# FFN up projection as seven products of halves, activations through DRAM, in a hybrid decoder layer on one NeuronCore

## The chip, the cores and the metric

The kernel runs on one core of a Trainium2 chip. The metric is device time in microseconds of one execution, the median of several runs. TensorE (PE) multiplies, VectorE (DVE) and ScalarE (ACT) do element-wise work, GpSimd (POOL) small scalars and some DMA issues, SyncE (SP) most DMA issues.

## The reference, cut

One decoder layer on 1024 tokens and 1024 channels in float32. Two sub-layers (a token mixer and a cross-attention into 256 memory tokens) come first and are not changed. The third is a gated MLP with a causal convolution of width 3 over the tokens:

```python
def conv_ffn(h, w_up, conv_w, conv_b, w_down):
    z = h @ w_up                                   # (1024 x 1024) @ (1024 x 5632)
    zc = conv_w[2] * z + conv_w[1] * shift_right(z, 1) + conv_w[0] * shift_right(z, 2) + conv_b
    g, u = zc[..., :D_FF], zc[..., D_FF:]          # D_FF = 2816
    return (jax.nn.gelu(g, approximate=True) * u) @ w_down

h = rms_norm(x, ffn_pre_g[l])
x = x + rms_norm(conv_ffn(h, w_up[l], conv_w[l], conv_b[l], w_down[l]), ffn_post_g[l])
```

## The kernel before

Every float32 product is made of three float32r matmuls: an operand is split into a rounded high part (`split`, L100, on ScalarE) and the rest (L101, on VectorE), and high x high, high x low and low x high are summed in PSUM.

The normalised activations are transposed to channels x tokens (`xtrans`, L894, through `transpose_pair`) into four tiles `h3` of the pool `hp`, a high and a low one for each half of the tokens. The pool has four buffers, and the cross-attention's output weights `woh`, `wol` hold two of them until its last product. The transposes of the last quarter of the tokens, `xtrans(3)`, come between the first up products (L975).

The up projection (L963 to L985) runs over j = 0 to 21, 128 gate columns and the 128 matching up columns of `w_up` each. `wload` fetches and splits a 128 x 1024 weight tile in the order of the list `stream`; `feature_major` (L226) multiplies it with both halves of the tokens over eight k tiles. The gate goes to one of two wide PSUM tiles, the up part to two of four banks. `conv_wide` and `conv` read PSUM: ScalarE makes the first tap and the bias, VectorE adds the other two. A gelu on ScalarE and a product on VectorE (L984, L985) give `act[j]`, and all 22 stay in SBUF in slots of the pool `ap` (28 slots of 4 KB per partition, shared by everything).

The down projection (L995 to L1176) already runs as seven products of halves (Strassen's scheme in Winograd's form): the tokens' halves, the halves of the 2816 and of the 1024 output columns. A step is one product and one of its eleven k tiles, 4 x 3 matmuls of 512 columns. `load` (L1032) fetches `w_down` four steps ahead, `prepare` (L1049) makes the sums and the split operands two steps ahead, `products` (L1082) issues the matmuls, `evacuate` empties the accumulators. The first two steps (HEAD = 2, L999) use tiles of the front pools; then these pools are closed (L1011) and the pool `dp` takes their place, so its tiles wait until their users are done.

The program text gives priorities; a planner in the framework orders each engine's queue by these and by when it expects inputs, so neighbouring instructions can change places. DMAs on one issuing queue start in order.

Of the kernel before, what the change touches and what calls it, by code (L numbers as in the profile page):

```python
# [16 lines left out]
P = 128  # L17
# [21 lines left out]
def hybrid_kernel(ctx, tc, out, x, xT, g_col, mem, gains, b_forget, w_fm, w_v0, w_v1, pool_w, pool_scale,  # L39
# [10 lines left out]
    ps = ctx.enter_context(tc.tile_pool(name="ps", bufs=4, space=bass.MemoryType.PSUM))  # L50
# [45 lines left out]
    def f32(a):  # L96
        return a.bitcast(F32)
# [20 lines left out]
    for j in range(NJ):  # L118
        stream += [w_up[j], w_up[NJ + j]]
# [772 lines left out]
    h3 = []  # L892

    def xtrans(q4, k2s=range(4)):  # L894
        if len(h3) <= q4 // 2:
            h3.append((hslot(), hslot()))
        c0 = (q4 % 2) * 256
        transpose_pair(yrs[q4], lambda k2: tuple(h3[q4 // 2][j][:, 2 * k2:2 * k2 + 2, c0:c0 + 256]
                                                 for j in range(2)), k2s, g_cols[:, 2])
# [21 lines left out]

    filler = xqueries(1)
    ox = xattend(0, lambda i: step(filler, 5))
    step(filler, 99)
    for q4 in range(4):
        units = xout(q4, ox)
        if q4 < 3:
            ox = xattend(q4 + 1, lambda i: step(units, 1))
        else:
            step(units, 6)  # L930
        if 0 < q4:
            xtrans(q4 - 1, (0, 1))
        step(units, 1)
        if 0 < q4:
            xtrans(q4 - 1, (2, 3))
        step(units, 9)


    act = [slot(s="act") for _ in range(NJ)]
    cg = [slot(s="cg") for _ in range(2)]  # L940

    ring(q=(0, 1), u=(2, 3, 0, 1))

    def conv(dst, o, m, hf, zt):

        w0, w1, w2 = (cwt[:, i, m:m + 1] for i in range(3))
        b, d = o[hf], dst[:, hf * 512:(hf + 1) * 512]
        nc.scalar.activation(d, b, AF.Identity, bias=cbt[:, m:m + 1], scale=w2)
        nc.vector.scalar_tensor_tensor(d[:, 1:], b[:, :511], w1, d[:, 1:], ALU.mult, ALU.add)
        nc.vector.scalar_tensor_tensor(d[:, 2:], b[:, :510], w0, d[:, 2:], ALU.mult, ALU.add)  # L950
        if hf == 0:
            nc.vector.tensor_copy(zt, b[:, 510:512])
        else:
            nc.vector.scalar_tensor_tensor(d[:, 0:1], zt[:, 1:2], w1, d[:, 0:1], ALU.mult, ALU.add)
            nc.vector.scalar_tensor_tensor(d[:, 0:2], zt, w0, d[:, 0:2], ALU.mult, ALU.add)

    def conv_wide(dst, b, m):
        w0, w1, w2 = (cwt[:, i, m:m + 1] for i in range(3))
        nc.scalar.activation(dst, b, AF.Identity, bias=cbt[:, m:m + 1], scale=w2)
        nc.vector.scalar_tensor_tensor(dst[:, 1:], b[:, :S - 1], w1, dst[:, 1:], ALU.mult, ALU.add)  # L960
        nc.vector.scalar_tensor_tensor(dst[:, 2:], b[:, :S - 2], w0, dst[:, 2:], ALU.mult, ALU.add)

    for j in range(NJ):  # L963
        gt, ut = cg[j % 2], act[j]
        wg = wload()
        wu = wload()
        og = wbank()
        ou = [bank("u"), bank("u")]
        zt = small(2, s="zt")
        if j == 0:  # L970
            for hf in range(2):
                feature_major(wg, h3, halves(og), (hf,))
                feature_major(wu, h3, ou, (hf,))
                if hf == 0:
                    xtrans(3)  # L975
                conv(ut, ou, NJ + j, hf, zt)
            conv_wide(gt, og, j)
        else:
            feature_major(wg, h3, halves(og))
            conv_wide(gt, og, j)  # L980
            feature_major(wu, h3, ou)
            for hf in range(2):
                conv(ut, ou, NJ + j, hf, zt)
        nc.scalar.activation(gt, gt, AF.Gelu_apprx_tanh)  # L984
        nc.vector.tensor_mul(ut, ut, gt)  # L985
# [5 lines left out]

    HEAD = 2  # L995
    operands = {}
    raw = new_raw().rearrange("p (k n) -> p k n", k=2)
    nc.sync.dma_start(out=raw, in_=w_down[0:2 * P, 0:512].rearrange("(k p) n -> p k n", p=P))
    for i in range(HEAD):  # L999
        o = []  # L1000
        for src in (act[i][:, :512], raw[:, i]):
            hi, lo = (wp.tile([P, 512], F32R, tag=t, name=nm(t), bufs=4) for t in ("wh", "wl"))
            split(hi, lo, src)
            o.append((hi, lo))
        operands[i] = o
        for t in range(4):
            tt = slice(t * P, (t + 1) * P)
            for n, (l, r) in enumerate(((0, 0), (0, 1), (1, 0))):
                nc.tensor.matmul(halves(wide[t // 2])[t % 2], o[0][l][:, tt], o[1][r], start=n == i == 0,
                                 stop=False, skip_group_check=True)  # L1010
# [6 lines left out]
    def residual(tg):  # L1017
# [8 lines left out]
    raws = {}  # L1026
    sums_a, sums_b = [], []

    NEEDS = {"p1": ((0, 0), (0, 1)), "p5": ((1, 1),), "p6": (), "p3": ((1, 1),),
             "p7": ((1, 1), (0, 1)), "p2": ((1, 0),), "p4": ()}  # L1030

    def load(i):  # L1032

        p, k = steps[i]
        if k % 2:
            return
        n = min(2, NK - k)
        for q in NEEDS[p]:
            r = dslot("wd", bufs=4)
            r0 = (q[0] * NK + k) * P  # L1040
            nc.sync.dma_start(out=r[:, :n], in_=w_down[r0:r0 + n * P, q[1] * 512:(q[1] + 1) * 512]
                              .rearrange("(k p) n -> p k n", p=P))
            for kk in range(n):
                raws[p, k + kk, q] = r[:, kk]

    def quarter(a, b, k):
        return act[b * NK + k][:, a * 512:(a + 1) * 512]

    def prepare(i):  # L1049

        p, k = steps[i]
        w = [raws.pop((p, k, q)) for q in NEEDS[p]] or [None]
        a11, a12, a21, a22 = (quarter(i, j, k) for i in range(2) for j in range(2))
        if p == "p1" and k % 2 == 0:
            sums_a.append(dslot("sa"))
            sums_b.append(dslot("sb"))
        s_, t_ = sums_a[k // 2][:, k % 2], sums_b[k // 2][:, k % 2]
        if p == "p7":
            nc.vector.tensor_tensor(w[0], w[0], w[1], ALU.subtract)
        a, b = {"p1": (a11, w[0]), "p5": (s_, t_), "p6": (s_, t_), "p3": (s_, w[0]),  # L1060
                "p7": (s_, w[0]), "p2": (a12, w[0]), "p4": (a22, t_)}[p]
        if i >= HEAD:
            o = [dslot("o", F32R) if i < tail else slot((P, 2, 512), F32R, s="ot") for _ in range(2)]
            split(o[0][:, 0], o[0][:, 1], a)
            split(o[1][:, 0], o[1][:, 1], b)
            operands[i] = o
        if p == "p1":
            nc.vector.tensor_tensor(s_, a21, a22, ALU.add)
            nc.vector.tensor_tensor(t_, w[1], w[0], ALU.subtract)
        elif p == "p5":  # L1070
            nc.vector.tensor_tensor(s_, s_, a11, ALU.subtract)
# [5 lines left out]
        elif p == "p2":  # L1077
            nc.vector.tensor_tensor(t_, w[0], t_, ALU.subtract)
# [165 lines left out]
```

## Time and profile before

| | |
|---|---|
| runs | 1552.12, 1557.56, 1558.25 us, median 1557.56 |
| profiled execution | 1554.77 us, span 1553.0 us |
| TensorE busy | 1514.1 us (97%) |
| VectorE busy | 893.8 us (58%) |
| ScalarE busy | 630.5 us (41%) |
| DMA | 131.17 MB, mean 84 GB/s |

The busy time of overlapping, pipelined matmuls says that TensorE has work, not that it runs at its peak; the spacing of matmul starts tells their pace. The up projection lies from about 840 to 1322 us of the span, the down projection behind it.

### The profile page before, as it was taken

How to read it: one execution, taken by the hardware profiler on the slowest of the kernel's cores; microseconds unless marked ns; L12 is line 12 of the kernel's file. 1: busy time of each engine (PE TensorE's matmuls, PEld its weight loads, DVE VectorE, ACT ScalarE, POOL GpSimd, SP SyncE). 2: the span in 40 equal slices, each digit the busy share in tenths (PEclk: the TensorE clock that was granted, in tenths of full speed). 3: DMA queues.
4: the chain of work that ended last, by engine and by line, in shares of the span. 5: the costliest groups of instructions: out<-in, count | busy, mean ns of one | idle time of the engine just before them, and what ended most of it. 6: DMA issues, size and time to landing. Idle time of an engine off the chain costs nothing. (4 is left out here: it accounts for less than half of the span.)

```text
span 1553.0 us, 19127 instructions
## 1 busy us (share of the span) xinstructions
PE 1514.1 (97%) x7316; PEld 1256.4 (81%) x7316; DVE 893.8 (58%) x1414; ACT 630.5 (41%) x1176; POOL 118.4 (8%) x270
## 2 busy tenths in 40 slices
PE   7999999999999999999999999999999999899997
PEld 7888888878888888877888888888888888688885
DVE  7578777663233444676565534444344444886786
ACT  6356555232122233554677322222232222354453
POOL 4000000000000000033022000000000000000003
PEclk9999999999999999999999999999999999899999
DMA  5244332111122125354222111111111111522622
GB/s 166 80 109 104 90 89 69 58 37 49 45 65 74 48 88 183 101 181 153 82 101 91 54 41 55 45 51 54 41 55 41 55 43 39 186 79 85 193 89 108
DMA packets 50315, 131.17 MB, mean 84 GB/s; under 512 B 6192, under 2 KB 6640, under 8 KB 50224
## 3 DMA queue, kind: packets, MB, share of 16 engines
q1 hardware_dynamic: 41824, 100.30, 21.7%
q0 software_dynamic: 8256, 29.40, 5.5%
q8 instruction: 57, 0.93, 0.3%
q14 instruction: 34, 0.28, 0.1%
q10 hardware_dynamic: 144, 0.26, 0.0%
HBM read 104.61 MB, written 12.75 MB: 76 GB/s over the span
## 5 line engine op out<-in xcount | busy, mean ns | idle before, releaser
L100 ACT ACTIVATE wh<-wr 128x512 fp32r<-128x512 f32 x214 | 134.0, 630 | 496.6 <-PE wide L235 292.4
L101 DVE TENSOR_TENSOR wl<-wr,wh 128x512 fp32r<-128x512 f32 x214 | 146.4, 689 | 306.2 <-ACT wh L100 306.0
L233 PE MATMUL wide<-h,wh 128*128 128x512 f32 x608 | 189.3, 390 | 0.9 <-ACT h L223 0.4
L237 PE MATMUL wide<-h,wl 128*128 128x512 f32 x608 | 189.2, 389 | 0.5 <-DVE wl L101 0.5
L235 PE MATMUL wide<-h,wh 128*128 128x512 f32 x608 | 189.0, 390 | 0.1
L233 PEld LDWEIGHTS wide<-h,wh 128*128 128x128 f32 x608 | 113.8, 188 | 25.6 <-ACT wh L100 0.7
L237 PEld LDWEIGHTS wide<-h,wl 128*128 128x128 f32 x608 | 114.1, 188 | 24.6 <-DVE wl L101 0.9
L235 PEld LDWEIGHTS wide<-h,wh 128*128 128x128 f32 x608 | 114.1, 188 | 24.4 <-DVE h L224 0.5
L1089 PE MATMUL wide<-o,o 128*128 128x512 f32 x456 | 106.9, 396 | 7.0 <-ACT o L100 6.9
L233 PE MATMUL bank<-h,wh 128*128 128x512 f32 x352 | 109.8, 389 | 0.0
L237 PE MATMUL bank<-h,wl 128*128 128x512 f32 x352 | 109.7, 389 | 0.0
L235 PE MATMUL bank<-h,wh 128*128 128x512 f32 x352 | 109.6, 389 | 0.0
L1089 PEld LDWEIGHTS wide<-o,o 128*128 128x128 f32 x456 | 87.2, 191 | 26.2 <-ACT o L100 7.3
L1089 PE MATMUL bank<-o,o 128*128 128x512 f32 x396 | 90.8, 390 | 0.0
L1089 PEld LDWEIGHTS bank<-o,o 128*128 128x128 f32 x396 | 74.1, 188 | 16.3 <-DVE o L101 0.9
L164 PE MATMUL bank<-h,wh 128*128 128x512 f32 x192 | 77.0, 401 | 1.3 <-DVE qk L442 1.3
L235 PEld LDWEIGHTS bank<-h,wh 128*128 128x128 f32 x352 | 66.1, 188 | 13.7
L237 PEld LDWEIGHTS bank<-h,wl 128*128 128x128 f32 x352 | 66.1, 188 | 13.7
L233 PEld LDWEIGHTS bank<-h,wh 128*128 128x128 f32 x352 | 66.1, 188 | 13.7
L165 PE MATMUL bank<-h,wh 128*128 128x512 f32 x192 | 76.0, 396 | 0.0
L166 PE MATMUL bank<-h,wl 128*128 128x512 f32 x192 | 75.8, 395 | 0.0
L101 DVE TENSOR_TENSOR pt<-bank,pt 128x512 fp32r<-128x512 f32 (+2 forms) x96 | 50.8, 550 | 11.0 <-ACT pt L100 10.7
(316 smaller groups left out, 2946.2 us busy)
## 6 DMA issues: line engine op xcount, KB each, us to landing
wr<-in_w_up SPq DMA_DIRECT2D x44, 512.0 KB
wd<-in_w_down SPq DMA_DIRECT2D x35, 512.0 KB
wr<-in_w_fm SPq DMA_DIRECT2D x28, 512.0 KB
wr<-in_w_mix_out SPq DMA_DIRECT2D x16, 512.0 KB
qs<-qk SPq DMA_DIRECT2D x32, 128.0 KB
kd<-qk SPq DMA_DIRECT2D x32, 128.0 KB
xr<-in_x POOLq DMA_DIRECT2D x8, 512.0 KB, 6.3
x1d<-xr POOLq DMA_DIRECT2D x8, 512.0 KB, 3.4
```

Of the source, the lines that this page charges most:

```text
L100: nc.scalar.activation(hi, src, AF.Copy)
L101: nc.vector.tensor_tensor(lo, src, f32(hi), ALU.subtract)
L164: nc.tensor.matmul(o, lh, rh, start=start, stop=False)
L165: nc.tensor.matmul(o, lh, rl, start=False, stop=False)
L166: nc.tensor.matmul(o, ll, rh, start=False, stop=stop)
L233: nc.tensor.matmul(o[h], wh[:, ks], hT[h][0][:, k], start=st, stop=False)
L235: nc.tensor.matmul(o[h], wh[:, ks], hT[h][1][:, k], start=False, stop=False)
L237: nc.tensor.matmul(o[h], wl[:, ks], hT[h][0][:, k], start=False, stop=sp)
L1089: nc.tensor.matmul(o, oa[:, l, tt], ob[:, r], start=n == k == 0 and p in ("p1", "p5", "p2"), stop=n == 2 and k == NK - 1, skip_group_check ...
```

## The change

The up projection gets the scheme that the down projection has. For each j, the 2 x 2 blocks are: gate or up columns, halves of the 1024 input channels, halves of the tokens. Seven products of a 128 x 512 weight block with a 512 x 512 activation block take the place of eight. The weight sums s1 to s4 are made by VectorE for each j (`prepare_up`, four products ahead); the activation sums t1 to t4 are made once (`b_sums`), in two quarters, from the right half's raw transposes `raws_b`, while p1 and p2 of the first three j, which need the left half only, run first. PSUM is laid out anew as eight banks, three for X (p1, p6, p7, p4 of one j accumulate there), three for p2, two for p5 and p3. Products are emptied by ScalarE (p1, p5, p6, p4) or added by VectorE (p3, p7, p2) into SBUF tiles, and the convolution reads those. `act[j]` and, for each pair, the sum of its right halves are written to DRAM on the POOL queue; the down projection loads the quarter it needs, pairs of neighbouring j being its two halves.

```diff
-    for j in range(NJ):
-        stream += [w_up[j], w_up[NJ + j]]
...
+    FILL = 3
+    up_steps = [(j, p) for j in range(FILL) for p in ("p1", "p2")]
+    for j in range(NJ):
+        up_steps += [(j, p) for p in ("p5", "p6", "p3", "p7")]
+
+        if j > 0:
+            at = up_steps.index((j, "p5")) + (1 if j < FILL else 0)
+            up_steps.insert(at, (j - 1, "p4"))
+        if j >= FILL:
+            up_steps.append((j, "p2"))
+        if FILL <= j + 1 < NJ:
+            up_steps.append((j + 1, "p1"))
+    up_steps.append((NJ - 1, "p4"))
+    LEAD_UP = 4
...
+    def prepare_up():
...
+        if name == "s1":
+            nc.vector.tensor_tensor(s_, a["a21"], a["a22"], ALU.add)
+        elif name == "s2":
+            nc.vector.tensor_tensor(s_, s_, a["a11"], ALU.subtract)
+        elif name == "s4":
+            nc.vector.tensor_tensor(s_, a["a12"], s_, ALU.subtract)
+        elif name == "s3":
+            nc.vector.tensor_tensor(s_, a["a11"], a["a21"], ALU.subtract)
+        hi, lo = up_ops[n % 6]
+        split(hi, lo, a.get(name, s_))
...
+    def b_sums(q4):
+
+        c = slice((q4 % 2) * 256, (q4 % 2) * 256 + 256)
+        r12, r22 = raws_b[q4]
+        t_ = slot((P, 4, 256), s="tr")
+        b11, b21 = quarters["b11"], quarters["b21"]
+        nc.vector.tensor_tensor(t_, r12, f32(b11[:, :4, c]), ALU.subtract)
+        nc.vector.tensor_tensor(t_, t_, f32(b11[:, 4:, c]), ALU.subtract)
+        b_split(q4, "t1", t_)
+        yield
+        nc.vector.tensor_tensor(t_, r22, t_, ALU.subtract)
+        b_split(q4, "t2", t_)
+        yield
+        b_split(q4, "b22", r22)
+        yield
+        nc.vector.tensor_tensor(r12, r22, r12, ALU.subtract)
+        b_split(q4, "t3", r12)
+        yield
+        nc.vector.tensor_tensor(t_, f32(b21[:, :4, c]), t_, ALU.subtract)
+        nc.vector.tensor_tensor(t_, t_, f32(b21[:, 4:, c]), ALU.add)
+        b_split(q4, "t4", t_)
+        yield
...
+    def product_up(n):
+        j, p = up_steps[n]
+        o = {"p5": UY[j % 2], "p3": UY[j % 2], "p2": UZ[j % 3]}.get(p, UX[j % 3])
...
+        for k in range(4):
+            ks = slice(k * P, (k + 1) * P)
+            for i, (l, r) in enumerate(((ah, bh), (ah, bl), (al, bh))):
+                nc.tensor.matmul(o, l[:, ks], r[k // 2][:, k % 2], start=i == k == 0 and p in ("p1", "p5", "p2"),
+                                 stop=i == 2 and k == 3, skip_group_check=True)
...
+    def pair_done(j):
+
+        d = conv_wide(z[j][1], NJ + j)
+        nc.vector.tensor_mul(d, d, gates.pop(j))
+        nc.gpsimd.dma_start(out=act_d[j], in_=d)
...
+        if j % 2:
+            s_ = slot((P, 512), s="sd")
+            nc.vector.tensor_tensor(s_, act_ring.pop(j - 1)[:, right], act_ring.pop(j)[:, right], ALU.add)
+            nc.gpsimd.dma_start(out=sum_d[j // 2], in_=s_)
...
+    plan = {0: ((2, 1),), 1: ((2, 2),), 2: ((3, 1),), 3: ((3, 1),), 4: ((3, 1),), 5: ((2, 1), (3, 1)), 6: ((2, 1), (3, 1))}
...
+    for n in range(len(up_steps)):
+        j, p = up_steps[n]
+        if n == 2:
+            xtrans(3)
+        product_up(n)
+        for q4, m in plan.get(n, ()):
+            step(sums[q4], m)
+        prepare_up()
...
-    HEAD = 2
+    HEAD = 4
...
+    LOADS = {"p1": ("a11", "b11"), "p5": ("s", "b12"), "p6": ("b22", "a12"), "p3": ("b22", "a21"),
+             "p7": ("b22", "b12"), "p2": ("b21",), "p4": ("a22",)}
...
+            if q == "s":
+                r = dslot("sa")
+                for kk in range(n):
+                    nc.sync.dma_start(out=r[:, kk], in_=sum_d[k + kk])
+            elif q[0] == "a":
+                r = slot((P, 2, 512), s=q)
+                c = slice((int(q[1]) - 1) * 512, int(q[1]) * 512)
+                for kk in range(n):
+                    nc.sync.dma_start(out=r[:, kk], in_=act_d[2 * (k + kk) + int(q[2]) - 1][:, c])
```

## Rows read from the trace of the kernel before

**Rows 1.** The page: busy time, share and instructions by engine; granted clock by slice.

```profile
PE 1514.1 (97%) x7316; PEld 1256.4 (81%) x7316; DVE 893.8 (58%) x1414; ACT 630.5 (41%) x1176; POOL 118.4 (8%) x270
...
PEclk9999999999999999999999999999999999899999
```

**Rows 2.** Windows, up then down: length, busy by engine (count), clock, DMA share, GB/s.

```profile
1000.00:1100.00 100.00, 100.00 (x443) 82.79 (x442) 44.42 (x62) 27.76 (x37) 0.00 (x0) 1.00 0.16 48
...
1360.00:1400.00 40.00, 40.00 (x178) 33.13 (x177) 34.27 (x55) 20.86 (x38) 0.00 (x0) 1.00 0.23 73
1400.00:1500.00 100.00, 100.00 (x441) 82.08 (x440) 77.77 (x127) 50.00 (x94) 4.31 (x8) 1.00 0.43 137
```

**Rows 3.** Timeline, up projection: start, duration, engine, line; one j apart.

```profile
1082.75 0.62 PE L233 MATMUL wide<-h,wh 128*128 128x512 f32 x2
...
1104.51 0.62 PE L233 MATMUL wide<-h,wh 128*128 128x512 f32 x2
```

**Rows 4.** Timeline of TensorE: hand-over, then whole products of the down projection.

```profile
1322.11 0.39 PE L1009 MATMUL wide<-wh,wh 128*128 128x512 f32 x1
...
1334.59 27.63 PE L1089 MATMUL wide<-o,o 128*128 128x512 f32 x108 [6.88 <-ACT o L100]
...
1362.05 30.08 PE L1089 MATMUL bank<-o,o 128*128 128x512 f32 x132
1391.97 30.08 PE L1089 MATMUL wide<-o,o 128*128 128x512 f32 x132
```

**Rows 5.** Instructions by line and form, down projection: busy us, mean ns, idle before.

```profile
L101 DVE TENSOR_TENSOR o<-sa,o 128x512 fp32r<-128x512 f32 x43 | 29.7, 690 | 18.1 <-ACT o L100 18.1
...
L1076 DVE TENSOR_TENSOR sa<-act 128x512 f32<-128x512 f32 x11 | 7.5, 684 | 0.0
...
L1113 DVE TENSOR_TENSOR y<-y,bank 128x512 f32<-128x512 f32 x4 | 2.5, 678 | 0.0
...
L100 ACT ACTIVATE o<-sa 128x512 fp32r<-128x512 f32 x43 | 27.2, 632 | 60.9 <-PE bank L1089 30.9 <-PE wide L1089 29.8
...
L1105 ACT ACTIVATE y<-wide 128x512 f32<-128x512 f32 x4 | 2.2, 589 | 0.2 <-PE wide L1089 0.2
```

**Rows 6.** Instructions by line and form, up projection, 880 to 1320.

```profile
L961 DVE SCALAR_TENSOR_TENSOR cg<-wide,cwt,cg 128x1022 f32<-128x1022 f32 x21 | 26.9, 1281 | 0.8
...
L985 DVE TENSOR_TENSOR act<-act,cg 128x1024 f32<-128x1024 f32 x20 | 24.5, 1226 | 0.7
L959 ACT ACTIVATE cg<-wide,cbt,cwt 128x1024 f32<-128x1024 f32 x20 | 23.8, 1191 | 0.0
L984 ACT ACTIVATE cg<-cg 128x1024 f32<-128x1024 f32 x21 | 22.3, 1061 | 57.5 <-DVE cg L961 57.5
```

**Rows 7.** Timeline of VectorE in the down projection: consecutive instructions.

```profile
1369.57 0.68 DVE L1071 TENSOR_TENSOR sa<-sa,act 128x512 f32<-128x512 f32 x1
...
1370.17 0.68 DVE L1072 TENSOR_TENSOR sb<-wd,sb 128x512 f32<-128x512 f32 x1
```

**Rows 8.** Timeline of TensorE: first up matmul, transposes of quarter 2.

```profile
839.64 0.39 PE L233 MATMUL wide<-h,wh 128*128 128x512 f32 x1
...
845.08 1.03 PE L215 MATMUL bank<-ident,y 128*128 128x128 f32 x8
```

**Rows 9.** Windows at the start of the up projection.

```profile
846.00:852.00 6.00, 6.00 (x31) 4.95 (x30) 1.80 (x4) 2.73 (x6) 0.19 (x1) 1.00 0.14 56
```

**Rows 10.** Windows at the hand-over to the down projection.

```profile
1334.50:1340.00 5.50, 5.29 (x12) 3.81 (x13) 5.11 (x9) 2.23 (x5) 0.00 (x0) 0.50 0.79 224
...
1345.00:1350.00 5.00, 5.00 (x23) 4.14 (x23) 4.31 (x8) 2.31 (x4) 0.00 (x0) 1.00 0.88 286
```

**Rows 11.** Timeline at the hand-over: loads issued, first split that waited.

```profile
1327.74 40.76 SPq L1041 DMA_DIRECT2D wd<-in_w_down  x17
...
1333.90 0.63 ACT L100 ACTIVATE o<-wd 128x512 fp32r<-128x512 f32 x1 [9.56 <-DMA wd<-in_w_down]
```

**Rows 12.** DMA issues: queue, count, size, median us to landing.

```profile
x2d<-xr POOLq DMA_DIRECT2D x8, 512.0 KB, 3.0
```

## Prediction of the time after the change

> **What bounds the kernel now.** I read the page's busy line and its 40 slices first [rows 1]: TensorE is busy 1514.1 of 1553.0 us at full clock nearly throughout, VectorE 893.8, ScalarE 630.5. So time is won by taking matmuls away, provided nothing else becomes late. Then the windows by stage [rows 2]: in the up projection TensorE is busy 100.00 of 100 us and VectorE only 44; in the down projection, which already runs as seven products, TensorE is at 100.00 with VectorE at 78, and in 1360 to 1400 at 34.27 of 40, which is 86%. This is the nearest thing the trace has to the up projection after the change: a Strassen stage with VectorE heavily used and TensorE without a gap.
>
> **TensorE in the up projection.** Before, each j issues 8 k x 3 x 4 halves = 96 matmuls of 512 columns. Two starts of the same matmul one j apart, 1082.75 and 1104.51, are 21.76 us apart [rows 3], so one matmul costs 0.2267 us. The down projection, with twelve matmuls to a product, has the same pace: 132 matmuls from 1362.05 to 1391.97 are 29.92 us, again 0.2267 [rows 4]. After, each j issues 7 products x 4 k x 3 = 84. Removed: 22 x 12 = 264 matmuls x 0.2267 = 59.8 us, all on the path since TensorE has no idle time there. A j then lasts 84 x 0.2267 = 19.04 us and one product 2.72 us.
>
> **VectorE in a j after the change.** Durations [rows 5, 6]: seven lo splits at 0.69 (4.83), four weight sums at 0.68 (2.74), three additions out of PSUM for p3, p7 and p2 at 0.68 (2.03), four convolution steps at 1.28 (5.12), the product of the branches 1.23, half a sum for DRAM 0.34: 16.3 us. Consecutive instructions start 0.08 us before the last one's recorded end (0.60 against 0.68) [rows 7], so about 19 instructions really take 14.8 us, 78% of 19.04. ScalarE: seven hi splits at 0.63, four evacuations at 0.59, two convolution starts at 1.19, a gelu at 1.06: 10.2 us, 54%. Neither is the bound, and the 86% row above says that such a load can stay hidden. What could leak is order. p3 accumulates onto p5's bank and p7 onto p6's, so ScalarE's evacuation has one product, 2.72 us, in which to come; a hi split queued before it that waits for a VectorE sum would delay it. VectorE's bursts are a gate's two steps after p2 (2.6) and those of the other branch with the product and the sum after p4 (4.5 at most); the operands are made four products, 10.9 us, ahead, so a burst is covered. If that cover is gone, a whole burst of 4.5 per j shows, and 22 of them cost 99 us; this is a rival below. No row of before shows this queue, so I bound it between 0 (the 86% row) and 0.8 us a j, one hi split, 18 us; I take 2 us, near the row.
>
> **The start of the up projection.** This is what the change adds on the path. For the right half of the tokens it makes t1, t2, b22, t3 and t4: six differences of 1024 columns and ten lo splits per quarter, in VectorE time 6 x 1.15 + 10 x 0.605 = 13.0 us, two quarters 25.9 us. Durations are those of the 1024-wide product (1.23) and the splits less 0.08 [rows 5 to 7]. It saves 16 lo steps of L224. To be hidden they must fit under the six products p1 and p2 of j 0 to 2 that need only the left half, and what follows. Up matmuls begin at 839.64 [rows 8]. p4 of j=0, which needs t4, is the twelfth product: 11 x 2.72 = 29.9 us later, plus some 24 transposes at 0.13 us (eight are recorded in 1.03 us with overlap [rows 8]), 3.2 us: 33 us. In it VectorE has 25.9 for the sums, 7.9 for operands (eight splits, five sums), 3.0 for evacuations and 2.4 for the last normalisations: 39.2. Some 3 us can start earlier, because the quarter's transposes now go to free buffers and no longer wait for buffers that the cross-attention's output weights hold (the transposes of quarter 2 finish only at 845 now). That leaves 36 against 33, so 3 us late, and each set also has a wait from difference to hi split to lo split of about 0.7 us, one hi duration, where nothing fills it. With five such waits, 3.5 us. I take 7 us of TensorE idle, most of it before p7 and p4 of j=0 and p5 of j=1. Bounds: 0, if the planner starts the sums as the buffers come (VectorE is busy only 1.80 of 6 us in 846 to 852 [rows 9]), and 17, if both quarters wait for the second one's transposes. A gap can also bring the lower clock: after the 7 us gap at the hand-over TensorE ran at 0.50, the 1.2 GHz level, from 1334.5 to 1340 [rows 10].
>
> **The hand-over to the down projection.** Now the first two steps of p1 end at 1327.5, then TensorE stands 6.88 us for w_down and its split, and restarts at half clock [rows 4, 10]. p1 takes from 1322.11 to 1362.05, 39.94 us for a product that takes 29.92 elsewhere: 10.0 us lost. After, four steps of operands are kept in slots that come free while the last products run (t1's after p5 of j=21, five products earlier), so 10.9 us of TensorE work cover the loads into the new pool; before, the loads needed from 1327.7 to 1333.9, about 6 us [rows 11]. I take 3 us left of 10.0, a gain of 7; bounds are 10 and 0.
>
> **The down projection's new transfers.** Its matmuls, splits and tail stay; the sums of a21 and a22 in p1 go to the up stage, and the other sums are made 1024 wide, so VectorE has less to do here. New are 14 MB read back: in p1, p5, p6, p3 and p7 every pair of steps loads 1 MB (two pieces of 256 KB and 512 KB of weights, or the same of weights) in 2 x 2.72 = 5.44 us, that is 193 GB/s. In 1345 to 1350 the DMA engines moved 286 GB/s at a share of 0.88 [rows 10], so this fits with a third to spare, with loads four steps ahead. SP issues them in order, so a load that waits for a slot holds back the weights behind it, and then the splits wait. Bounds 0 and 6 (one late pair in each product at about 1.2); I take 1. Writes of act and of the sums go out on the POOL queue; a 512 KB write from there now lands 3.0 us later [rows 12]. POOL does nothing else in this stage and nobody waits for the data before the down projection, so nothing; if that cover failed, a late write would hold a slot and hence an evacuation, which is within the bound of the queue above.
>
> **Sum,** against the profiled execution's 1554.77 us (span 1553.0; 2.8 below the median of the runs, 1557.56, so about their lower half): 1554.8 - 59.8 + 2 + 7 - 7 + 1 = 1498.0. Of the part that is counted, 59.8 is sure as far as the pace holds; the other terms nearly cancel, and with all good ends the sum is 1554.8 - 59.8 - 10 = 1485; with all bad ones 1554.8 - 59.8 + 18 + 17 + 6 = 1536.
>
> **Rivals.** (1) VectorE and ScalarE lead in the up stage: the waits between sum, hi, lo and evacuation don't overlap and each j loses some 1.5 us, giving 22 x 1.5 = 33 us back: 1498 + 33 - 2 = 1529, and with a loss of 2.5 us a j about 1551, no change. For it: 78% and 54% busy with five changes of engine per product chain. Against it: the 86% row with no idle TensorE. (2) Slower than before: the down projection becomes bound by its transfers. There are 27.5 pairs of steps in the five heavy products. To lose the remaining gain of 57 us each must last 57 / 27.5 = 2.1 us longer, 7.5 us for 1 MB, so it decides from a rate below 140 GB/s; at 110 GB/s a pair lasts 9.5 us, +4.1 x 27.5 = 113 us, 1611. Against it: 224 GB/s and more where many loads were queued [rows 10]; for it: rows of 2 KB, pieces half as large, and one queue in order. The Trainium skill (DMA: Bandwidth & Descriptors, Anatomy of one DMA) speaks against the change here: a fixed 2.0 us for each DMA besides bytes over 436 GB/s, with half the rate only at about 860 KB; an estimate from it, pieces taken one after the other, is 2.6 + 2.6 + 3.2 = 8.4 us a pair and about +81 us. The trace agrees on one transfer (3.0 us for 512 KB [rows 12]) and not on the queue, since 286 GB/s in [rows 10] needs several in flight. (3) The start is hidden and the hand-over closes: 1485 to 1490, inside my range.
>
> **How the numbers follow.** The forecast, 1498, with rival 3, has 0.80 between 1485 and 1530. Rival 1 above that, up to 1547, has 0.08; near no change 0.05; rival 2 and any other cause of a slower kernel 0.07. The range is 1485 to 1532. Differences under 0.5% (7.8 us) cannot be told from no change. Faster: 0.80 + 0.08 = 0.88; same 0.05; slower 0.07.
>
> **What would show it.** Right: a spacing of 19.0 us between the same matmul of two j, TensorE at 100 in windows of 900 to 1250, VectorE at 75 to 86% there; idle of TensorE of 3 to 15 us within 40 us of the first up product, waiting for a split of t2, t3 or t4; p1 of the down projection in 30 to 34 us; the other products at 29.9. Wrong: idle before p3 or p7 that waits for ScalarE in every j; a spacing above 19.5; splits in the down projection that wait for loads of act for more than 1 us at a time; the lower clock in more than one stretch.

## The result and the profile of the changed kernel

| | before | changed |
|---|---|---|
| median of the runs | 1556.98 us | 1530.66 us (1530.06 to 1532.50) |
| profiled execution | 1554.77 us, span 1553.0 | 1532.5 us, span 1530.4 |
| ratio to before | | 0.9839, 95% interval 0.9816 to 0.9861 |

The kernel is 26 us faster; 57 were forecast. The time lies inside the range, but less than half of the gain came. The busy line of its page (busy us by engine, share of the span, instructions) answers to [rows 1]:

```profile
PE 1470.9 (96%) x7052; PEld 1210.3 (79%) x7052; DVE 1024.6 (67%) x1505; ACT 718.0 (47%) x1328; POOL 135.8 (9%) x303
```

and the windows by stage (length, busy time by engine with counts, granted clock, DMA share, GB/s) to [rows 2]:

```profile
880.00:890.00 10.00, 7.94 (x32) 5.57 (x31) 10.00 (x15) 3.77 (x8) 0.00 (x0) 1.00 0.19 54
890.00:900.00 10.00, 9.15 (x38) 6.80 (x38) 9.99 (x15) 6.62 (x10) 0.00 (x0) 1.00 0.16 52
1000.00:1100.00 100.00, 100.00 (x435) 81.20 (x434) 80.35 (x103) 49.64 (x74) 3.75 (x7) 1.00 0.26 85
1100.00:1200.00 100.00, 100.00 (x434) 80.97 (x433) 77.90 (x101) 50.42 (x74) 4.29 (x8) 1.00 0.28 92
1400.00:1500.00 100.00, 98.81 (x431) 80.29 (x430) 81.66 (x119) 52.97 (x104) 11.32 (x19) 1.00 0.46 151
```

Three things are to be seen. In the middle of the up projection TensorE has no gap and VectorE is at 78 to 80%, as forecast; but only 435 and 434 matmuls fit into 100 us where the kernel before has 443 in the same windows, so each takes longer than 0.2267 us. At the start (880 to 900) VectorE is full and TensorE is not. The down projection runs nearly as before, from its 49th matmul to its last in 201.0 us where it was 200.1: its transfers don't bound it.

The start, by waits (TensorE, 838 to 925; us in total, times, longest):

```profile
PE acc L914 <- ACT y L206: 6.4, 1, 6.4
PE acc L1094 <- ACT t L101: 2.5, 1, 2.5
PE acc L1094 <- DVE wl L102: 1.6, 2, 1.0
```

and in two windows of it, from the first up matmul, 843.93, to the transposes of the last quarter, 856.16, and from there to the 13th product, 897.45:

```profile
843.93:856.16 12.23, 5.85 (x29) 4.55 (x27) 6.00 (x5) 6.54 (x13) 4.68 (x7) 0.95 0.11 44
856.16:897.45 41.29, 35.53 (x136) 26.97 (x136) 37.40 (x52) 24.24 (x46) 0.00 (x0) 0.89 0.08 26
```

TensorE waits 6.4 us for the normalised rows of the last quarter (y) and then again and again for sums. Twelve products and the transposes are 12 x 2.72 + some 2 = 34.6 us of TensorE; they took 53.5. So 18.9 us were lost. Part of them went at the lower of the clock's two levels, 1.2 GHz: the granted clock was 0.52 from 856 to 862, behind the gap of 6.4 us, and 0.83 from 870 to 880, where TensorE waits 2.5 us for t; from 862 to 870 and from 880 to 900 it was 1.00.

The hand-over (timeline; answers to [rows 4, 11]):

```profile
1291.39 1.40 SPq L1206 DMA_DIRECT2D sb<-in_w_down  x3
...
1293.55 0.83 SPq L1201 DMA_DIRECT2D a<-act  x2
...
1300.06 0.63 ACT L101 ACTIVATE ot<-a 128x512 fp32r<-128x512 f32 x1 [5.69 <-DMA a<-act]
...
1302.03 0.63 ACT L101 ACTIVATE ot<-b 128x512 fp32r<-128x512 f32 x1 [1.34 <-DMA b<-in_w_down]
...
1302.71 14.21 PE L1263 MATMUL acc<-ot,ot 128*128 128x512 f32 x48 [11.35 <-ACT ot L101]
...
1316.76 8.57 PE L1263 MATMUL acc<-o,o 128*128 128x512 f32 x37
```

The last up matmul starts at 1290.97. Only then, at 1291.39, does SP issue the first loads of the new stage, and these are three sb tiles for later steps; the a and b of the first step follow at 1293.55 and 1294.56. TensorE stands still for 11.35 us and then takes 14.05 us for 48 matmuls (10.9 at 0.2267). From the last up matmul to the 97th of the new stage it is 36.7 us where 97 x 0.2267 = 22.0 are needed: 14.7 lost, against 10.0 before. In the windows there the transfers are at work and the granted clock is at the lower level:

```profile
1296.00:1302.00 6.00, 0.00 (x0) 0.00 (x0) 2.61 (x3) 0.63 (x1) 1.07 (x2) 0.50 1.02 334
1302.00:1308.00 6.00, 5.29 (x12) 3.89 (x13) 3.21 (x6) 3.62 (x7) 0.00 (x0) 0.50 1.04 407
```

Last, the pitch, which is the time from the start of one matmul to the start of the next. Timeline of TensorE, where the moving operand changes from t4 to t1 (at 1003.05):

```profile
1001.69 0.62 PE L1094 MATMUL acc<-t,wh 128*128 128x512 f32 x2
...
1002.37 0.62 PE L1094 MATMUL acc<-t,wh 128*128 128x512 f32 x2
...
1003.05 0.63 PE L1094 MATMUL acc<-t,wh 128*128 128x512 f32 x2
...
1003.75 0.63 PE L1094 MATMUL acc<-t,wh 128*128 128x512 f32 x2
```

Three matmuls lie between the first two rows, 0.68 / 3 = 0.2267 us each; three between the last two, 0.70 / 3 = 0.2333. The switch falls on the boundary of a product. Over the whole stage each combination of a product and an operand buffer has a pitch of its own that recurs to within a nanosecond or so (p4 with the first three buffers: 226.7 ns, three times each; p5 with the same ones: 233.5 to 233.6). The DMA share and busy ScalarE or VectorE hardly go with it (correlations of 0.3, 0.0 and 0.2 over stretches of 15 matmuls). What does is where the tiles lie. No view of the trace shows addresses; by those of the built program the tiles t1, t2 and b22 and the fifth and sixth operand buffer (uo) start at multiples of 64 bytes, and all tiles on the right side of SBUF (b11, b21, t3, t4, wh, wl) 32 bytes past one. Take the steps between matmuls of one product after the first 300 matmuls, without nine steps of over 0.3 us: the 756 with both operands at the same offset have a mean of 228.1 ns (median 227), and the 654 with different ones 233.0 (median 233). In all, 864 of the 1848 mix offsets; in the up and down projections before, none did.

### The profile page after: what moved, and what is told of

Same layout as the page of the kernel before. It is cut to its first block, busy times and chain, and to the rows that moved or that the text cites. A ratio compares the mean times of both kernels' runs of the same rounds, so it can differ in the third digit from the quotient of the medians.

```text
span 1530.4 us, 19075 instructions
## 1 busy us (share of the span) xinstructions
PE 1470.9 (96%) x7052; PEld 1210.3 (79%) x7052; DVE 1024.6 (67%) x1505; ACT 718.0 (47%) x1328; POOL 135.8 (9%) x303
## 4 chain that ended last, share of the span: by engine, by line
PE 83%; DVE 5%; DMA 5%; ACT 3%; issue 2%; POOL 2%; SPq 1%; DVEq 0%; ACTq 0%; POOLq 0%
PE acc L1094 27%; PE acc L1263 10%; PE bank L163 7%; PE bank L165 7%; PE bank L164 7%; PE wide L232 4%; PE wide L236 4%; PE wide L234 4%; PE bank L554 3%; PE wide L163 3%; PE wide L165 2%; PE wide L164 2%; PE bank L543 2%; DMA wd<-in_w_down 2%; PE wide L459 1%
## 5 line engine op out<-in xcount | busy, mean ns | idle before, releaser
L1263 PE MATMUL acc<-o,o 128*128 128x512 f32 x828 | 189.3, 390 | 1.2 <-DVE o L102 1.0
L1263 PEld LDWEIGHTS acc<-o,o 128*128 128x128 f32 x828 | 155.0, 188 | 35.3 <-DVE o L102 3.2
L1094 PE MATMUL acc<-t,wh 128*128 128x512 f32 x464 | 146.9, 397 | 3.3 <-ACT t L101 2.5
L1094 PE MATMUL acc<-b,wh 128*128 128x512 f32 x368 | 116.1, 397 | 0.0
L1094 PEld LDWEIGHTS acc<-t,wh 128*128 128x128 f32 x464 | 87.5, 190 | 25.3 <-ACT t L101 2.9
L1094 PE MATMUL acc<-t,wl 128*128 128x512 f32 x232 | 91.8, 396 | 1.0 <-DVE wl L102 1.0
L236 PE MATMUL wide<-h,wl 128*128 128x512 f32 x256 | 79.6, 390 | 1.1 <-DVE wl L102 1.1
L232 PE MATMUL wide<-h,wh 128*128 128x512 f32 x256 | 79.5, 391 | 0.5 <-ACT wh L101 0.3
L234 PE MATMUL wide<-h,wh 128*128 128x512 f32 x256 | 79.2, 390 | 0.0
L163 PE MATMUL bank<-h,wh 128*128 128x512 f32 x192 | 77.0, 401 | 1.3 <-DVE qk L441 1.3
L164 PE MATMUL bank<-h,wh 128*128 128x512 f32 x192 | 76.0, 396 | 0.0
L165 PE MATMUL bank<-h,wl 128*128 128x512 f32 x192 | 75.8, 395 | 0.0
```

Of the source, the lines that this page charges most:

```text
L163: nc.tensor.matmul(o, lh, rh, start=start, stop=False)
L164: nc.tensor.matmul(o, lh, rl, start=False, stop=False)
L165: nc.tensor.matmul(o, ll, rh, start=False, stop=stop)
L232: nc.tensor.matmul(o[h], wh[:, ks], hT[h][0][:, k], start=st, stop=False)
L234: nc.tensor.matmul(o[h], wh[:, ks], hT[h][1][:, k], start=False, stop=False)
L236: nc.tensor.matmul(o[h], wl[:, ks], hT[h][0][:, k], start=False, stop=sp)
```

## The experiments

All times below are medians; before was 1555.7 to 1556.9 in the same sessions, the changed kernel 1530.7. "Start" is the time from the first up matmul to that of the 13th product (53.5 us in the changed kernel), "hand-over" that from the last up matmul to the 97th of the down projection (36.7 us).

### One offset for all operands

```diff
     front = ctx.enter_context(ExitStack())
+    pad = ctx.enter_context(tc.tile_pool(name="pad", bufs=1, side="right"))
+    nc.vector.memset(pad.tile([P, 8], F32, tag="pad", name="pad8"), 0.0)
     hp = front.enter_context(tc.tile_pool(name="hp", bufs=4, side="right"))
     wp = front.enter_context(tc.tile_pool(name="wp", bufs=2, side="right"))
```

> Edit: 32 unused bytes ahead of the buffers on the right side of SBUF, so that the stationary and the moving operand of every matmul lie at the same offset within 64 bytes (in the changed kernel 864 of the 1848 matmuls of the up projection mix offsets 0 and 32). Nothing else moves. Theory 1 (placement sets the pace): every product of the up projection runs at 0.2267 us a matmul, a j lasts 19.04 us in place of 19.35, 864 x 0.0066 = 5.7 us go in this stage, and some more where the front of the kernel mixes offsets (1492 matmuls, mostly narrower): 1521 to 1526 us. Theory 2 (transfers, ScalarE or VectorE beside it slow TensorE): products between 0.2267 and 0.2336 as now, 1530 us within 2.

1519.59 us; ratio to before 0.9763 (0.9746 to 0.9779), where the changed kernel has 0.9839. The window of the up projection:

```profile
1000.00:1100.00 100.00, 100.00 (x441) 82.19 (x440) 80.83 (x105) 48.81 (x72) 4.28 (x8) 1.00 0.27 90
```

441 matmuls in place of 435, with VectorE, ScalarE and the transfers as busy as before. From the 21st product on the mean pitch is 0.2275 in place of 0.2310 us, 5.6 us for the stage. The rest, some 5 us, comes from the front of the kernel, more than I had expected there (the first up matmul starts at 838.54 in place of 843.93); the next run prices it. Theory 2, load on other engines, falls. What is left above 0.2267 is one step of some 0.34 us inside p3 of every other j, about 1.3 us in the stage; the changed kernel has it too, and its cause is open.

### The kernel before, with one offset

The same edit in the kernel before.

> Edit: the kernel before with the same 32 unused bytes ahead of its right-hand buffers. Its up and down projections already have both operands at one offset, while 1492 matmuls of the parts ahead of them mix offsets. If offsets set the pace, the up and down stages keep 0.2267 us and only the front gets shorter: 1549 to 1553 us in place of 1556; if the gain of the aligned changed kernel came from elsewhere in the up stage, no change, 1555 to 1557.

1551.31 us, ratio 0.9964 (0.9954 to 0.9975): the front alone gains 5.6 us here (the first up matmul starts at 834.75 in place of 839.64), and the up projection keeps its pitch of 0.2267 us. If it gains as much in the changed kernel, about half of the 11 us is a loss that the change brought and half one that it found.

### The kernel before, with mixed offsets

The reverse: in the kernel before, the same 32 bytes between the two right-hand pools.

```diff
     hp = front.enter_context(tc.tile_pool(name="hp", bufs=4, side="right"))
+    pad = front.enter_context(tc.tile_pool(name="pad", bufs=1, side="right"))
+    nc.vector.memset(pad.tile([P, 8], F32, tag="pad", name="pad8"), 0.0)
     wp = front.enter_context(tc.tile_pool(name="wp", bufs=2, side="right"))
```

> Edit: the kernel before with 32 unused bytes between the pool of its transposed activations and the pool of its split weights, so that all 2880 matmuls of its wide products (2112 of them in the up projection) mix offsets 32 and 0, which none did; 240 others no longer do. If offsets set the pace: a matmul of the up projection takes 0.2333 in place of 0.2267, a j 22.4 in place of 21.76 us, the stage +14 and the front about +4, 1573 to 1577 us. If they don't: 1555 to 1558.

1572.78 us, ratio 1.0100 (1.0085 to 1.0115).

```profile
1000.00:1100.00 100.00, 100.00 (x430) 80.37 (x429) 44.43 (x66) 26.68 (x36) 0.00 (x0) 1.00 0.15 48
```

430 matmuls in place of 443 [rows 2], 0.2333 us each, with VectorE at 44% as before. 32 unused bytes cost this kernel 16 us. Apart from one small memset the padding moves only addresses, so where the operands lie sets the pitch; this is shown in both directions.

### The loads of the hand-over in the order of need

```diff
-                nc.sync.dma_start(out=r[:, :n], in_=w_pairs[...][:, k:k + n, c])
+                dma = nc.sync.dma_start(out=r[:, :n], in_=w_pairs[...][:, k:k + n, c])
+                if i < 2 * NK:
+                    in_order(dma)
```

and likewise for the loads of act and sum.

> Edit: the loads of the down projection's first two products are issued on SP in the order in which they are needed, so the first a11 and b11 stand ahead of the sb, sa and later ones that wait for a buffer of the up stage. Theory 1 (the queue's order makes the hand-over late): the first loads start while the last up products run, TensorE's gap of 11.35 us at 1302.7 shrinks to 3 to 5, and the first 48 matmuls of the down projection run near full clock (11 to 12 us in place of 14.05): 1519 to 1524 us. Theory 2 (the first buffers come free no earlier, whatever stands ahead): gap of 9 us or more, 1528 to 1532.

1527.46 us: 3 us, half of the least that theory 1 gave. Timeline of this run:

```profile
1280.59 0.80 SPq L1201 DMA_DIRECT2D a<-act  x2
...
1293.70 1.06 ACT L1125 ACTIVATE d<-d 128x1024 f32<-128x1024 f32 x1
...
1294.67 0.61 ACT L101 ACTIVATE ot<-a 128x512 fp32r<-128x512 f32 x1
...
1295.01 1.28 DVE L1118 SCALAR_TENSOR_TENSOR d<-zu,cwt,d 128x1022 f32<-128x1022 f32 x1
...
1295.85 0.73 PE L1267 MATMUL acc<-ot,ot 128*128 128x512 f32 x1 [4.11 <-ACT ot L101]
...
1298.27 0.68 DVE L102 TENSOR_TENSOR ot<-a,ot 128x512 fp32r<-128x512 f32 x1
...
1299.61 12.46 PE L1267 MATMUL acc<-ot,ot 128*128 128x512 f32 x47 [3.02 <-DVE ot L102]
```

The first loads are now issued more than ten us before the last up matmul (1291.36) and are no longer late; the first matmul of the new stage comes 4.5 us after the last one of the old, not 11.7. It waits 4.11 us for high splits: on ScalarE the last j's evacuation, first tap and gelu (1291.8 to 1294.8) stand ahead of them, and the first split starts at 1294.67, right behind the gelu. The second matmul waits 3.02 us for a low split: on VectorE the convolution, product and sum of the last j (1291 to 1298) stand ahead of all splits. The hand-over is 31.4 us. Two more queues stood behind the first.

### Loads and first splits ahead of the last j's tail

On top of the edit before:

```diff
+        if n == len(up_steps) - 3:
+            load(0)
+            load(2)
+        if n == len(up_steps) - 1:
+            prepare(0)
+            prepare(1)
         if p == "p4":
             pair_done(j)
```

> Edit: as in the run with the loads in order, and besides, the loads of the down projection's first four steps are issued three up products before the end, and the splits of its first two steps are queued on ScalarE and VectorE ahead of the last j's convolution, product and sum. Theory 1 (after the loads, VectorE's queue is what is late: the last j's 7 us of tail stand before the first low splits): TensorE's gap of 4.1 + 3.0 us falls under 2 in total, the first 96 matmuls of the down projection end 25 us or less after the last up matmul (36.7 in the changed kernel, 31.4 with the loads in order, 22 without any loss): 1519 to 1523 us. Theory 2 (the loads' waits for buffers hold it): gap of 4 or more remains, 1526 to 1529.

1519.72 us, ratio 0.9767 (0.9753 to 0.9782).

```profile
1289.95 1.19 PE L1273 MATMUL acc<-ot,ot 128*128 128x512 f32 x4 [0.38 <-ACT ot L101]
...
1292.49 0.68 DVE L102 TENSOR_TENSOR ot<-a,ot 128x512 fp32r<-128x512 f32 x1
...
1292.63 5.73 PE L1273 MATMUL acc<-ot,ot 128*128 128x512 f32 x24 [1.48 <-DVE ot L102]
...
1299.60 4.83 PE L1273 MATMUL acc<-ot,ot 128*128 128x512 f32 x20 [1.24 <-DVE ot L102]
```

The gap is gone (0.38 us) and 1.48 and 1.24 us are left, both for low splits on VectorE, where the last j's tail now stands between the second and the third step. The hand-over takes 26.0 us, 10.7 less than in the changed kernel. Theory 1 is right, with one thing added: queues in order made the hand-over late, SP's first, and behind it ScalarE's as well as VectorE's, since the edit moves the splits ahead on both. The buffers were free.

### The last quarter's transposes two products later

```diff
-        if n == 2:
+        if n == 4:
             xtrans(3)
```

with the sums of the last quarter two products later in the plan.

> Edit: the transposes of the last quarter stand behind four up products in place of two, and its sums move two products back. Theory 1 (TensorE waits for the last quarter's rows, which come 12 us after the first up product): the gap of 6.38 us at 856 falls under 1.5 and the low clock behind it goes: 1522 to 1526 us. Theory 2 (VectorE, full from 860 to 900, sets when t1 to t4 are there): the gap goes but comes back as waits for t1, t2, t3, t4 of the last quarter, 1529 to 1533; the start of p6 of j=1, now 53.5 us after the first up product, moves by under 2.

1529.82 us (1525.85 to 1533.47). Waits of TensorE and two windows of this run:

```profile
PE acc L1094 <- ACT t L101: 5.0, 1, 5.0
PE acc L1094 <- ACT uo L101: 2.1, 1, 2.1
PE acc L914 <- ACT y L206: 0.9, 1, 0.9
```

```profile
870.00:880.00 10.00, 8.97 (x29) 6.89 (x30) 10.00 (x16) 6.67 (x12) 0.00 (x0) 0.72 0.16 50
880.00:890.00 10.00, 9.18 (x39) 6.89 (x38) 10.00 (x13) 3.89 (x7) 0.00 (x0) 1.00 0.20 56
```

The wait for y falls from 6.4 to 0.9 us and comes back as 5.0 for t and 2.1 for an operand, with VectorE full. The start is 51.1 us, 2.4 less. Theory 2 in the main, though it had the start move by under 2; the runs lie too far apart for the time to decide.

### The last rows first on ScalarE

```diff
+            with tc.high_priority() if tg == NT - 1 else ExitStack():
                 ss = small()
                 nc.scalar.activation(y, b, AF.Square, accum_out=ss)
```

> Edit: the last row tile's normalisation after the cross-attention is given priority, which puts its Square ahead of one scaling and three copies on ScalarE (about 2 us of work). Theory 1 (ScalarE's queue makes the last rows late): they come 2 us sooner, the gap of 6.38 us falls to about 4.4: 1528 to 1529 us. Theory 2 (the chain from Square to the last scaling, 8.8 us, waits for something else, or VectorE sets the end): 1530 to 1531.

1527.44 us; the wait for y is 3.9 us in place of 6.4 and the start 50.0 in place of 53.5. Theory 1. That 3.5 us came for a wait that is 2.5 shorter would fit rows that also let VectorE begin sooner, which a later transpose doesn't; this is argued, not shown.

### VectorE's work at the start, less of it

Two runs take work away from VectorE. Both leave out a part of the arithmetic, so they are measurements and not versions to keep.

```diff
-        nc.vector.tensor_tensor(t_, t_, f32(b11[:, 4:, c]), ALU.subtract)
...
-        nc.vector.tensor_tensor(t_, t_, f32(b21[:, 4:, c]), ALU.add)
```

> Edit: the changed kernel without the two VectorE instructions per quarter that take the low parts of b11 and b21 into t1, t2 and t4 of the right half (4 x 1.15 = 4.6 us of VectorE; three of the four come after 855 us). This leaves out a part of the sums, so that the right half's sums have the precision of the high parts alone. Theory 1 (VectorE's load sets the start): the 13th product starts 3 to 4.6 us sooner than 53.5 after the first, 1526 to 1528 us. Theory 2 (other waits set it): under 1 us, 1530 to 1531.

1524.80 us; start 47.8 us, 5.7 sooner for 4.6 us of work, more than theory 1 had. The wait for y is 5.5 us here in place of 6.4.

```diff
-            split(hi[i][:, :, c], lo[i][:, :, c], src[:, 2 * i:2 * i + 2])
+            nc.scalar.activation(hi[i][:, :, c], src[:, 2 * i:2 * i + 2], AF.Copy)
+            nc.gpsimd.memset(f32(lo[i][:, :, c]), 0.0)
```

> Edit: the changed kernel with the twenty low parts of t1, t2, b22, t3 and t4 of the right half set to zero by GpSimd in place of being subtracted on VectorE (20 x 0.6 = 12 us of VectorE). This leaves these low parts out, so that the right half's operands have the precision of the high parts alone. Theory 1 (VectorE's amount of work sets the start): the 13th product starts 9 to 12 us sooner, 42 to 45 us after the first, what is left being the wait for the last rows (6.4): 1519 to 1522 us. Theory 2 (the chain of difference, high part and wait sets it): the high parts' chain stays, 3 to 5 us sooner, 1526 to 1528.

1521.81 us; start 44.7 us, 8.8 sooner. All waits of TensorE between 833 and 900 in this run:

```profile
PE acc L914 <- ACT y L206: 6.4, 1, 6.4
PE bank L914 <- ACT rb L917: 0.6, 1, 0.6
```

Every wait for a sum is gone; what is left is the wait for the last rows and the low clock behind it (0.54 from 854 to 860). So of the lost 18.9 us, 8.8 go with VectorE's work, theory 1, and about 10 remain (44.7 - 34.6). Two things keep this from being a clean split. The shares don't add: when the wait for the rows was all but removed, with VectorE's work in place, only 2.4 us went. And the longest wait for a sum in the changed kernel, for the high part of t1, came while VectorE itself was idle and waited for ScalarE:

```profile
873.12 0.69 DVE L102 TENSOR_TENSOR wl<-su,wh 128x512 fp32r<-128x512 f32 x1 [2.81 <-ACT wh L101]
...
874.18 0.49 PE L1094 MATMUL acc<-t,wh 128*128 128x512 f32 x1 [2.46 <-ACT t L101]
```

There the order on ScalarE, where the evacuation of the last quarter's transposes (868.99) and the split of b22 stand ahead of t1's, came last. In the run above these transposes start 21.7 us after the first up matmul, in the changed kernel 24.4. So VectorE's amount of work is shown to matter; that it alone makes the 8.8 us is not.

### Work of the start on GpSimd

```diff
-            split(hi[i][:, :, c], lo[i][:, :, c], src[:, 2 * i:2 * i + 2])
+            split(hi[i][:, :, c], lo[i][:, :, c], src[:, 2 * i:2 * i + 2], nc.gpsimd)
```

> Edit: the twenty low parts of t1, t2, b22, t3 and t4 of the right half are subtracted on GpSimd, which is idle there, in place of VectorE (20 x 0.6 = 12 us of VectorE work at the start of the up projection). Theory 1 (VectorE's load sets the start): the start of the 13th product, 53.5 us after the first one, comes 5 to 9 us sooner, and VectorE is no longer full from 880 to 900: 1522 to 1526 us. Theory 2 (the late rows of the last quarter set it): under 2 us, 1529 to 1531. Theory 3 (GpSimd takes over 1.5 us for a subtraction and is itself late): slower than 1531.

1540.11 us, 9.4 slower than the changed kernel: theory 3. The start takes 61.4 us, 7.9 longer. The first up matmul comes 3.5 us later too (847.4), though nothing ahead of it was edited, and the hand-over is 2.0 shorter. Instructions by line and form, GpSimd from 840 to 910 and VectorE from 845 to 905:

```profile
L102 POOL TENSOR_TENSOR t<-tr,t 128x512 fp32r<-128x512 f32 x12 | 19.4, 1638 | 9.1 <-ACT t L101 9.1
L102 POOL TENSOR_TENSOR b<-rb,b 128x512 fp32r<-128x512 f32 x4 | 7.1, 1792 | 0.3 <-ACT b L101 0.3
...
L102 DVE TENSOR_TENSOR wl<-su,wh 128x512 fp32r<-128x512 f32 x5 | 5.6, 1116 | 0.0
L1109 DVE TENSOR_TENSOR zg<-zg,acc 128x512 f32<-128x512 f32 x3 | 2.0, 679 | 2.1 <-ACT zg L1098 2.1
```

GpSimd takes 1.64 to 1.79 us for what VectorE does in 0.68. And VectorE itself becomes slow: its splits from SBUF take 1.12 us on average in place of 0.68, while its additions out of PSUM (L1109) stay at 0.68. The Trainium skill bears on both (GPSIMD Engine Reference, Architecture: its ports to SBUF are shared with VectorE; Engine selection: about half VectorE's speed for two inputs). The trace agrees: GpSimd takes 2.4 to 2.6 times as long, and what slows on VectorE has both inputs in SBUF, while the additions out of PSUM don't slow.

### The four edits together, and then without GpSimd

> Edit: the changed kernel with one offset for all operands, the loads and first splits of the down projection early, the last rows' normalisation with priority and the low parts of the right half's sums on GpSimd. If the four losses are separate, the gains add: about 11 for the offsets, 8 to 11 for the hand-over, 3 for the last rows and 5 for VectorE's relief, 1530.7 - 28 = 1503 us (1500 to 1507); if they overlap (a start that is late anyhow), 1507 to 1513.

1515.34 us: above both theories. The gains do add, 11 + 11 + 3, but the fourth edit, taken for a gain of 5 before its own run was known, costs 9: 1530.7 - 25 + 9.4 = 1515. Without GpSimd:

> Edit: the changed kernel with one offset for all operands, the early loads and first splits of the down projection and the priority of the last rows' normalisation; the low parts stay on VectorE. If the gains are separate they add: 11.4 + 11 + 3, 1530.7 - 25.4 = 1505 us (1502 to 1508), below both kernels; the start of the up projection stays the largest loss, 13th product 49 to 50 us after the first.

1506.93 us, ratio to before 0.9684 (0.9668 to 0.9700): the three gains are separate. And with the later transposes besides:

> Edit: the same with the last quarter's transposes behind four up products. Theory 1 (the wait for the rows is a loss of its own): the rest of the gap, 3.9 us, goes, 1501 to 1504 us. Theory 2 (VectorE sets the end of the start, so that a wait that is removed comes back later): within 1.5 us of the run without it.

1505.34 us, ratio 0.9672 (0.9658 to 0.9687). The start ends at 887.44 us here and at 887.49 without the edit, both with a span of 1503.5. Theory 2 again: at most 1.6 us, within the spread of the runs. This is the fastest version.

### Only t3 on GpSimd

```diff
-        nc.vector.tensor_tensor(r12, r22, r12, ALU.subtract)
-        b_split(q4, "t3", r12)
+        nc.gpsimd.tensor_tensor(r12, r22, r12, ALU.subtract)
+        b_split(q4, "t3", r12, nc.gpsimd)
```

> Edit: the best version so far with the last quarter's transposes later, and the difference for t3 and its low parts on GpSimd (VectorE has 2 x 1.15 + 4 x 0.6 = 4.7 us less to do; GpSimd some 2 x 3.3 + 4 x 1.7 = 13.4 us, worked out from the 1.64 to 1.79 us that it took for 512 columns). Theory 1 (VectorE's amount sets the start, and t3, needed last but one, can come late): 1505.3 - 4 = 1501 us (1500 to 1503). Theory 2 (GpSimd's t3 is late for the tenth product): 1505 or more.

1508.61 us, 3.3 slower than without it.

```profile
862.71 4.41 POOL L1075 TENSOR_TENSOR rb<-rb,rb 128x1024 f32<-128x1024 f32 x1 [12.03 <-ACT rb L920]
...
867.15 0.63 ACT L103 ACTIVATE t<-rb 128x512 fp32r<-128x512 f32 x1 [3.16 <-POOL rb L1075]
867.69 1.13 ACT L103 ACTIVATE t<-tr 128x512 fp32r<-128x512 f32 x2
...
868.33 3.04 DVE L104 TENSOR_TENSOR t<-tr,t 128x512 fp32r<-128x512 f32 x2 [2.82 <-ACT t L103]
...
868.35 0.80 PE L1097 MATMUL acc<-t,wh 128*128 128x512 f32 x1 [6.68 <-ACT t L103]
```

Theory 2, but not as I had put it: t3 isn't late for its own product. Its high split waits on ScalarE for GpSimd (3.16 us), the high split of t1 is queued behind it, and p5 waits 6.68 us for that. And VectorE's two splits of t1 take 3.04 us while GpSimd runs, in place of 1.28 in the changed kernel.

## Why the prediction was wrong

Its terms against the trace, in the prediction's order:

- **Matmuls taken away, -59.8.** The mechanism is right: 264 fewer, all on the path. Only the clause "as far as the pace holds" failed. The pitch of 0.2267 came from stages [rows 3, 4] in which both operands of every matmul have the same offset; the change moved nearly half of the stage's matmuls (864) to pairs of tiles with different ones. No view of the trace names an address, but the list of slots in the diff does: t1, t2, b22 and uo are new on the other side of SBUF.
- **Steady queue, +2 (0 to 18).** The order held: TensorE waits for nothing between 900 and 1290, with VectorE at 78 to 80% and ScalarE at 50% in the windows above (78 and 54 forecast). Rival 1 was wrong. (0.2310 - 0.2267) x 1607 matmuls = 6.9 us are lost all the same, nearly all by the offsets: 5.6 of them go with 32 bytes. A j lasts 19.4 us on average, where 19.0 was the sign of being right and 19.5 that of being wrong.
- **Start, +7 (0 to 17).** 18.9, outside the bounds. VectorE's work was well sized: 43.4 us in the trace to the 13th product, 39.2 reckoned to the 12th. The failed step is the comparison of two totals, 36 us against 33, which lets VectorE work from the first moment on. The sums of the last quarter can't begin before its rows, and its high parts queue on ScalarE. Up to 856.16 VectorE had 6.0 of 12.2 us to do, and 37.4 were left for ten products of 27.2. I had also placed the last rows' end in the shade of the products, and their 6.4 us were in no bound.
- **Hand-over, -7 (10 to 3 left).** 14.7 left, worse than before and outside the bounds. "10.9 us of TensorE work cover the loads" holds only if the loads are issued in that time. Slots were free, but on SP loads that waited for the end of the stage stood ahead, the very risk that I named for the down projection's later loads and didn't apply here; and the last j's work on ScalarE and VectorE stood ahead of the splits. With all of it set right, 4.0 are left, where 3 were forecast.
- **Down transfers, +1 (0 to 6).** From the 49th matmul to the last it is 201.0 us where the kernel before took 200.1: 0.9, as forecast. Rival 2 fell: right behind the hand-over, from 1302 to 1330, the DMA engines moved 389 to 407 GB/s, well above the 286 of [rows 10]. The estimate of +81 us, for pieces taken one after the other, fell with it.
- **A term that was put at nothing: the tail.** "Its matmuls, splits and tail stay" left it out of the sum. From the last matmul to the end it is 12.7 us where it was 9.9. All transfers but one small one are over 5.4 us before the end, where it was 2.7 in the kernel before; what fills the difference is open.

Together, as differences of the two profiled spans: the forecast is 1553.0 - 56.8 = 1496.2, measured was 1530.4, 34.2 more. The first up matmul comes at 843.9 in place of 839.6, +4.3. From it to the last one it is 447.0 us where 482.2 - 59.8 + 2 + 7 = 431.4 were forecast, +15.6; from there to the last down matmul 226.8 where 221.3 - 7 + 1 = 215.3 were, +11.5; and the tail adds 2.8. (Start and steady queue, taken one by one, give 16.8, because the kernel before also lost some 1 to 2 us in its up projection.) Of the 4.3 us, 2.6 are transposes of quarter 2 that now stand ahead of the first up matmul (841.38 to 843.93); but in the runs whose front has no edit it lies anywhere from 840.3 to 847.4.

With the mended losses the kernel takes 1505.3; without the 5.6 us that the front gained besides it would be 1511, still 13 above the forecast. In its profiled span, 4.8 us too many lie in the up projection, where the start stays the largest loss (48.6 us where 34.6 + 7 were forecast), 0.6 in hand-over and down projection, 2.8 in the tail; the rest is the front.

## What to carry to other kernels

When a change moves an operand to another pool, look at the addresses: a pitch read from a stage holds for its pairs of tiles, not for the shape alone. Work that must fit under other work is to be compared from the moment its input exists, not over the whole stretch. And "the loads have time" is a claim about a queue: list what stands ahead of them on the engine that issues them, and then what stands ahead of the first instruction that uses them.

## What the runs showed of the hardware

- In the kernel before, a float32r matmul of 512 columns took 226.7 ns, start to start, with stationary and moving operand at the same offset (modulo 64 bytes, by the built program) and 233.3 ns with 32 bytes of padding between their pools; such padding made the kernel before 16 us slower or 5.6 us faster, depending on the place. Offsets other than 0 and 32 weren't tried.
- Subtractions of two SBUF tiles on GpSimd (1.42 to 1.79 us on average for 512 columns, 3.4 for 1024) slowed those on VectorE at the same time: 128 x 512 took as much as 1.77 us in place of 0.68. Additions with one operand in PSUM kept 0.68.
- A long gap of TensorE cost more than its length: after the 11.35 us at the hand-over the granted clock was 0.50 from 1302 to 1308, the 1.2 GHz level, and 48 matmuls took 14.05 in place of 10.9 us. With the loads and splits early, gaps of 0.38 to 1.48 us left the clock at 1.00 from 1288 to 1308.
